# x and the output moved in two transfers each, the first of a multiple of 16 rows, and a ninth buffer for x

## The chip, the cores and the metric

The kernel runs on one core of a Trainium2 chip. A core has a matrix engine (TensorE, PE in the profile, with its weight load as PEld), a vector engine (DVE), a scalar engine (ACT), GpSimd (POOL), and SyncE (SP), which here only issues transfers. Sixteen DMA engines move data between the chip's main memory (HBM) and the core's on-chip memory (SBUF). Each engine works off its own list of instructions in the order in which the program was built; engines wait for each other through semaphores. A DMA is issued by one engine's queue (SP, ACT or POOL) and then runs by itself.

The metric is the device time of one execution in microseconds, less is better.

## The reference

A decoder trunk with two layers over 16 learned meta tokens followed by 1024 tokens of x, model width 1024, all in float32. Layer 0 is a Mamba-2 mixer and a gated feed-forward with a short causal convolution; layer 1 is stick-breaking attention and the same kind of feed-forward. What stands at the two ends matters here:

```python
def reference(x, meta_tokens, ...):
    h = jnp.concatenate([meta_tokens[None], x], axis=1)        # 1040 rows of 1024
    ...
    h = h + _ssd_mixer(_rmsnorm(h, ssd_norm[layer]), ...)
    h = h + _conv_ffn(_rmsnorm(h, ffn_norm[layer]), ...)
    ...
    h = h + _stick_breaking_attention(q, k, v) @ sb_w_o
    h = h + _conv_ffn(...)
    return _rmsnorm(h, final_norm)[:, N_META:]                 # 1024 rows of 1024
```

## The kernel before

**Tiles.** The 1040 rows are cut into nine chunks `CH`: eight of 116 rows and a last one of 112. Three chunks make a token tile `TT` of 348 (or 344) columns. A chunk sits in SBUF with its rows on the partitions, 4 KB to a row. The first chunk is made of the 16 meta rows and 100 rows of x, so its load from x has 100 rows, and so has its store.

**The start (`load_x`, L279 to L350).** For each chunk a tile `x` is taken from a pool with `XB` buffers (L292, L51), and its load is issued on SP for odd chunks and on ACT for even ones (L293 to L297). The weight for dt (`w_dt`, L299) is loaded after the first chunk. Then `ORD` (L50) sets six steps in order: `stream` of token tile 0, `stream` of 1, `scaled` of 0 and so on.

- `stream(j)` squares its three chunks and sums each row (L316 on DVE for the chunks in `SQD`, that is 1, 4 and 7; L318 on ACT for the others). Then it goes through eight column blocks k: three transposes on TensorE (L323), a copy to `h` by ACT or DVE in turn (L326, L328), and the product for dt (L329), which the profile shows as a pair of matmuls. In token tile 2 each finished row block of `h` is stored to `h_d` on SP (L331). `token_rstd` (L195 to L209) makes 1/rms for each row.
- `scaled(j)` multiplies the three chunks by their 1/rms in place (L340), transposes them again (L345), and splits each result into a high and a low part (L256, L257). A chunk's buffer is free after its `scaled`.

The projections of the mixer follow: `load_w` (L135) loads a weight tile of 512 KB on SP (L138), splits it on ACT (L144) and POOL (L145), and `mm3` makes three matmuls for each pair of tiles (L151 to L153; in the projections their output is `pj`).

**The end (`finish`, L1419 to L1471).** It is called for each token tile when its rows of the last feed-forward are complete. It transposes the chunks back (L1432), multiplies by 1/rms and the gain (L1466 with L1467, or L1469), and stores each chunk of `y` on SP (L1471). For the last token tile the squares are taken after the transposes (L1450 to L1457).

**What sets the order.** Outside two stretches that are ordered by hand (the chunks of the state-space mixer and the attention), a planner sets the order of the instructions on each engine when the program is built: it runs the program through a simulated time line and writes down the order that comes out. SP's order, with all its transfers, comes from it in the whole program. The programs of before and after are each planned anew.

Of the kernel before, what the change touches and what calls it, by code (L numbers as in the profile page):

```python
# [16 lines left out]
META = 16  # L17
# [30 lines left out]
SUMS = ((6, 1), (3, 6), (7, 6), (3, 5), (5, 7)), ((4, 7), (2, 1))  # L48
LPOOL = ((2, 2), (2, 4), (2, 6), (2, 7))
ORD = ((0, 0), (1, 0), (0, 1), (1, 1), (0, 2), (1, 2))  # L50
XB, SQD = 8, (1, 4, 7)  # L51
SCALE = 0.125


# [12 lines left out]
class Trunk:  # L67
# [211 lines left out]
    def load_x(self, pool, mx):  # L279

        nc, a = self.nc, self.a
        H = HEADS
        ss = self.cp.tile([P, 9], F32, tag="ss0", name="ss0")
        nc.vector.memset(ss, 1.0)
        wdt = self.wp.tile([P, 1024], F32, tag="w32", name="wdt")
        self.ln_exp()
        d = self.dp.tile([KD, P, L], F32, tag="h0_d", name="h0_d")
        r9 = mx.tile([P, 3, 3], F32, tag="r9", name="r9")
        dt = self.ex("dtr")
        xs = []  # L290
        for c, (t0, n) in enumerate(CH):
            xt = pool.tile([P, D], F32, tag="x", name=self.nm("x"), bufs=XB)  # L292
            if c == 0:  # L293
                nc.sync.dma_start(xt[:META, :], a["meta"])
                nc.scalar.dma_start(xt[META:n, :], a["x"][: n - META, :])
            else:
                (nc.sync if c % 2 else nc.scalar).dma_start(xt[:n, :], a["x"][t0 - META : t0 - META + n, :])  # L297
            if c == 0:
                nc.sync.dma_start(wdt[:, : KD * H], a["w_dt"])  # L299
                v = wdt[:, : KD * H].rearrange("p (k h) -> p k h", k=KD)  # L300
                nc.gpsimd.tensor_tensor(v, v, self.par("ssd_norm", 0, KD).unsqueeze(2).to_broadcast([P, KD, H]), op=ALU.mult)
            xs.append(xt)
        u = [(self.Q("uh", F32R), self.Q("ul", F32R)) for _ in range(KD)]
        for t in (t for hl in u for t in hl):
            nc.gpsimd.tensor_copy(t[:, :HALO], self.zero)
        hs = [self.Q("h") for _ in range(KD)]

        def stream(j):
            s0, nn = TT[j]
            x3 = xs[3 * j : 3 * j + 3]  # L310
            for i in range(3):
                c = 3 * j + i
                n = CH[c][1]
                t = self.wp.tile([P, D], F32, tag="wl", name=self.nm("junk"))
                if c in SQD:
                    nc.vector.scalar_tensor_tensor(t[:n, :], x3[i][:n, :], 1.0, x3[i][:n, :], op0=ALU.mult, op1=ALU.mult, accum_out=ss[:n, c : c + 1])  # L316
                else:
                    nc.scalar.activation(t[:n, :], x3[i][:n, :], AF.Square, accum_out=ss[:n, c : c + 1])  # L318
            for k in range(KD):
                ps = self.lg("xT")  # L320
                for i in range(3):
                    n = CH[3 * j + i][1]
                    nc.tensor.transpose(ps[:, i * CB : i * CB + n], x3[i][:n, k * P : k * P + P], self.ident[:n, :n])  # L323
                h = hs[k][:, s0 : s0 + nn]
                if k % 2:
                    nc.scalar.activation(h, ps[:, :nn], AF.Copy)  # L326
                else:
                    nc.vector.tensor_copy(h, ps[:, :nn])  # L328
                nc.tensor.matmul(dt[j * H : j * H + H, :nn], wdt[:, k * H : k * H + H], h, start=k == 0, stop=k == KD - 1)  # L329
                if j == 2:  # L330
                    nc.sync.dma_start(d[k], hs[k][:, :L])  # L331
            self.token_rstd(ss[:, 3 * j : 3 * j + 3], CB, 3, y=r9[:, :, j])

        def scaled(j):
            s0, nn = TT[j]
            x3 = xs[3 * j : 3 * j + 3]
            for i, t in enumerate(x3):
                n = CH[3 * j + i][1]
                r = r9[:n, i : i + 1, j]
                nc.vector.tensor_scalar(t[:n, :], t[:n, :], r, None, op0=ALU.mult)  # L340
            for k in range(KD):
                ps = self.sm("xr")
                for i in range(3):
                    n = CH[3 * j + i][1]
                    nc.tensor.transpose(ps[:, i * CB : i * CB + n], x3[i][:n, k * P : k * P + P], self.ident[:n, :n])  # L345
                self.parts(ps[:, :nn], u[k], s0, nn, self.par("ssd_norm", k))

        for step, j in ORD:
            (scaled if step else stream)(j)
        return d, u, dt, r9  # L350

    def spill(self, rows, name):
        d = self.dp.tile([len(rows), P, L], F32, tag=name, name=name)
        for k, t in enumerate(rows):
            self.nc.gpsimd.dma_start(d[k], t[:, :L])
        return d
# [1062 lines left out]
    def finish(self, h, j):  # L1419
        nc, out = self.nc, self.a["out"]  # L1420
        if j == 0:
            self.gfin = self.wp.tile([P, D], F32, tag="w32", name="gfin")
            nc.sync.dma_start(self.gfin, self.a["final_norm"].to_broadcast([P, D]))
        s0, n = TT[j]
        chunks = [(i, *CH[3 * j + i]) for i in range(3)]
        ss = self.small("fs")
        banks = cycle((self.sm,) if j < 2 else (self.lg, self.mm, self.lg, self.ex, self.mm, self.ex))

        def flip(t0, m, b):
            p = next(banks)("fin")  # L1430
            for k in range(4):
                nc.tensor.transpose(p[:m, k * P : k * P + P], h[4 * b + k][:, t0 : t0 + m], self.ident)  # L1432
            return p

        if j < 2:
            accs = self.square_sum([h[k][:, s0 : s0 + n] for k in range(KD)], n, D)
            pss = self.sm("fs")
            for i, _, m in chunks:
                for x, acc in enumerate(accs):
                    nc.tensor.matmul(pss[:m, i : i + 1], acc[:, i * CB : i * CB + m], self.one, start=x == 0, stop=x == 1)  # L1440
            nc.vector.tensor_copy(ss[:CB, 0:3], pss[:CB, 0:3])
            r = self.token_rstd(ss, CB, 3, 0.0)
            flipped = {}
        else:
            s2 = self.cp.tile([P, 2, 4], F32, tag="fs2", name="fs2")
            nc.vector.memset(s2, 0.5 * D)
            flipped = {(i, b): flip(t0, m, b) for i, t0, m in chunks for b in range(2)}
            for i, _, m in chunks:
                for b in range(2):
                    p, q = flipped[i, b], self.wp.tile([P, D], F32, tag="wl", name=self.nm("junk"))[:m, :512]  # L1450
                    if b:
                        c = self.wp.tile([P, D], F32, tag="wh", name=self.nm("copy"))
                        nc.vector.tensor_copy(c[:m, :512], p[:m])
                        p = flipped[i, b] = c[:, :512]
                        nc.vector.scalar_tensor_tensor(q, p[:m], 1.0, p[:m], op0=ALU.mult, op1=ALU.mult, accum_out=s2[:m, b, i : i + 1])
                    else:
                        nc.scalar.activation(q, p[:m], AF.Square, accum_out=s2[:m, b, i : i + 1])  # L1457
            nc.vector.tensor_tensor(ss[:, :3], s2[:, 0, :3], s2[:, 1, :3], op=ALU.add)
            r = self.token_rstd(ss, CB, 3)
        for i, t0, m in chunks:  # L1460
            y = self.Q("y")[:, :D]
            for b in range(2):
                w = slice(512 * b, 512 * b + 512)
                p = flipped.get((i, b)) or flip(t0, m, b)
                if b and i < 2:
                    nc.scalar.activation(y[:m, w], p[:m], AF.Copy, scale=r[:m, i : i + 1])  # L1466
                    nc.gpsimd.tensor_tensor(y[:m, w], y[:m, w], self.gfin[:m, w], op=ALU.mult)  # L1467
                else:
                    nc.vector.scalar_tensor_tensor(y[:m, w], p[:m], r[:m, i : i + 1], self.gfin[:m, w], op0=ALU.mult, op1=ALU.mult)  # L1469
            s = META if t0 == 0 else 0  # L1470
            nc.sync.dma_start(out[t0 + s - META : t0 + m - META, :], y[s:m, :])  # L1471

    def run(self, ctx):
        tc = self.tc
# [84 lines left out]
```

## Time and profile before

| | us |
|---|---|
| median of 3 runs | 3035.69 |
| lowest and highest run | 3035.06, 3035.73 |
| the profiled execution | 3036.55 |
| its span, first to last instruction | 3034.8 |

Over the span TensorE is busy 95% (2885.8 us), its weight loads 91%, DVE 76%, ACT 54% and POOL 43%. The transfers moved 273.42 MB at a mean of 90 GB/s; the queue of SP carried 258.54 MB of that and the queue of ACT 6.56 MB.

The span is the profiler's, from the first to the last instruction; the execution's own time is 1.75 us longer. In the lines of the profile, `out<-in` names the tile written and the tiles read, `x3` counts instructions, and brackets give the idle time of the engine before the instruction and what ended it. A line that starts with two numbers has the start and the length in us. `SPq` and `ACTq` stand for transfers issued on those engines' queues: their time is that of the issue, not of the transfer. A line of the waits has who waited, for whom, the sum in us, how often, and the longest.

### The profile page before, as it was taken

Reading aid. Unit: us, or ns where it says so; the run is one execution under the profiler, and the core shown is the slowest. Engines: PE = TensorE matmul, PEld = TensorE weight load, DVE = VectorE, ACT = ScalarE, POOL = GpSimd, SP = SyncE. Lnnn points to the kernel's source line nnn. Section 1 sums busy time; section 2 is a strip of 40 time slices with the busy share of each in tenths; the row PEclk is TensorE's granted clock in tenths of the full one; section 3 lists DMA queues with packets and bytes.
Section 4 is the critical chain, followed back from the end, with each engine's and each line's share of the span. In section 5 each row is a group of like instructions: output and inputs, shape, how many; then the busy total and the mean of one; then the engine's idle time right before and its main releaser. Section 6 shows DMA issues by size and latency. Waiting matters only on the chain.

```text
span 3034.8 us, 58705 instructions
## 1 busy us (share of the span) xinstructions
PE 2885.8 (95%) x22535; PEld 2773.6 (91%) x22535; DVE 2307.4 (76%) x4062; ACT 1650.2 (54%) x3403; POOL 1310.5 (43%) x1257
## 2 busy tenths in 40 slices
PE   5999999989998999999999999999898999999997
PEld 2999898979998999998999999999798999999996
DVE  3677868886459878878876888888749888778874
ACT  2555545553235555565334888888736555655332
POOL 1154434452234766663443222222344666663441
PEclk8999999999999999999999999999999999999998
DMA  3333333323222222225232222221332222225231
GB/s 109 112 95 89 109 91 104 98 81 129 63 79 74 74 81 78 77 87 187 72 122 85 56 68 59 70 63 52 135 107 72 83 78 75 81 86 188 77 99 56
DMA packets 123221, 273.42 MB, mean 90 GB/s; under 512 B 13468, under 2 KB 53020, under 8 KB 122940
## 3 DMA queue, kind: packets, MB, share of 16 engines
q1 hardware_dynamic: 117622, 258.54, 27.6%
q10 hardware_dynamic: 4054, 6.56, 0.6%
q8 instruction: 177, 2.90, 0.4%
q0 software_dynamic: 1264, 4.57, 0.4%
q14 instruction: 104, 0.85, 0.1%
HBM read 201.25 MB, written 53.45 MB: 84 GB/s over the span
## 4 chain that ended last, share of the span: by engine, by line
PE 43%; DVE 7%; issue 2%; ACT 1%; POOL 0%; DMA 0%; POOLq 0%; DVEq 0%; ACTq 0%
PE p L152 5%; PE p L151 5%; PE p L153 5%; PE acc L152 4%; PE acc L153 4%; PE acc L151 4%; PE pj L151 3%; PE pj L153 3%; PE pj L152 3%; PE po L1329 3%; PE lg L1288 2%; PE wT L1315 2%; DVE gl L1025 2%; PE ms L801 0%; DVE p L1041 0%
## 5 line engine op out<-in xcount | busy, mean ns | idle before, releaser
L151 PE MATMUL pj<-uh,wh 128*128 128x348 f32 (+2 forms) x1536 | 505.1, 329 | 9.3 <-ACT bk L602 6.5
L152 PE MATMUL pj<-ul,wh 128*128 128x348 f32 (+2 forms) x1536 | 496.6, 323 | 0.0
L153 PE MATMUL pj<-uh,wl 128*128 128x348 f32 (+2 forms) x1536 | 494.9, 322 | 0.7 <-POOL wl L1180 0.7
L151 PE MATMUL p<-bh,fh 128*128 128x262 f32 x1408 | 403.8, 287 | 6.6 <-DVE c L276 4.5
L153 PE MATMUL p<-bh,fl 128*128 128x262 f32 x1408 | 403.0, 287 | 3.6 <-POOL fl L875 3.6
L152 PE MATMUL p<-bl,fh 128*128 128x262 f32 x1408 | 402.3, 286 | 0.1
L875 POOL TENSOR_TENSOR fl<-x,fh 128x1024 fp32r<-128x1024 f32 x88 | 212.5, 2416 | 269.6 <-ACT fh L874 174.1
L152 PE MATMUL p<-bl,wh 128*128 128x262 f32 x1056 | 303.1, 287 | 6.2 <-DVE bl L827 6.1
L151 PEld LDWEIGHTS pj<-uh,wh 128*128 128x128 f32 x1536 | 291.2, 190 | 15.1 <-issue 4.8
L151 PE MATMUL p<-bh,wh 128*128 128x262 f32 x1056 | 302.4, 287 | 0.9 <-ACT bh L826 0.9
L145 POOL TENSOR_TENSOR wl<-w,wh 128x1024 fp32r<-128x1024 f32 (+2 forms) x76 | 155.2, 2044 | 341.0 <-ACT wh L144 340.9
L153 PE MATMUL p<-bh,wl 128*128 128x262 f32 x1056 | 301.3, 285 | 0.0
L276 DVE SCALAR_TENSOR_TENSOR c<-p,params,c 128x260 f32<-128x260 f32 x528 | 251.6, 483 | 56.2 <-ACT c L273 46.6
L152 PEld LDWEIGHTS pj<-ul,wh 128*128 128x128 f32 x1536 | 291.6, 190 | 1.4 <-issue 0.7
L153 PEld LDWEIGHTS pj<-uh,wl 128*128 128x128 f32 x1536 | 291.0, 189 | 1.1 <-POOL wl L1180 1.0
L151 PEld LDWEIGHTS p<-bh,fh 128*128 128x128 f32 x1408 | 268.8, 191 | 7.5 <-ACT c L273 4.9
L153 PEld LDWEIGHTS p<-bh,fl 128*128 128x128 f32 x1408 | 268.4, 191 | 4.1 <-POOL fl L875 4.0
L152 PEld LDWEIGHTS p<-bl,fh 128*128 128x128 f32 x1408 | 268.7, 191 | 0.8 <-DVE bl L827 0.5
L152 PE MATMUL acc<-gl,wh 128*128 128x260 f32 x896 | 255.1, 286 | 11.7 <-DVE gl L1025 11.7
L151 PE MATMUL acc<-gh,wh 128*128 128x260 f32 x896 | 251.0, 285 | 8.8 <-DVE p L1070 7.6
L153 PE MATMUL acc<-gh,wl 128*128 128x260 f32 x896 | 253.6, 285 | 0.0
L916 DVE TENSOR_TENSOR c<-c,c 128x260 f32<-128x260 f32 x176 | 240.7, 1370 | 4.9 <-ACT c L912 1.9
(324 smaller groups left out, 8436.8 us busy)
## 6 DMA issues: line engine op xcount, KB each, us to landing
w<-in_w_up SPq DMA_DIRECT2D x88, 512.0 KB
g<-c SPq DMA_DIRECT2D x176, 130.0 KB
w<-in_w_down SPq DMA_DIRECT2D x44, 512.0 KB
w<-in_w_in SPq DMA_DIRECT2D x40, 512.0 KB
b<-g SPq DMA_DIRECT2D x32, 520.0 KB
E<-ea_d SPq DMA_DIRECT2D x32, 464.0 KB
D<-acs_d SPq DMA_DIRECT2D x32, 420.5 KB
h<-h_d SPq DMA_DIRECT2D x16, 520.0 KB
```

The source lines that it names most:

```text
L145: nc.gpsimd.tensor_tensor(wl[:, :n], w32[:, :n], wh[:, :n].bitcast(F32), op=ALU.subtract)
L151: mm(out, wh, uh, start=first, stop=False, skip_group_check=joins)
L152: mm(out, wh, ul, start=False, stop=False, skip_group_check=joins)
L153: mm(out, wl, uh, start=False, stop=last, skip_group_check=joins)
L276: nc.vector.scalar_tensor_tensor(out, ps[:, o + i : o + i + n], wcol(i), out, op0=ALU.mult, op1=ALU.add)
L875: tt(lo[:, :n], t, hi[:, :n].bitcast(F32), op=ALU.subtract)
L916: self.last_up = tt(g[:, :FN], g[:, :FN], v[:, :FN], op=ALU.mult)
L1025: tt(gl, x, gh.bitcast(F32), op=SUB)
L1288: nc.tensor.matmul(ps[:nt, :m], part[:, c0 : c0 + nt], ks[a][:, s0 : s0 + m], start=x == 0, stop=x == 1)
L1315: nc.tensor.transpose(pt[:ns, x * CB : x * CB + nt], bt[a][:nt, x * CB : x * CB + ns], self.ident[:nt, :nt])
L1329: nc.tensor.matmul(po[64 * a : 64 * a + 64, :nt], v[: CH[c][1], c, 64 * a : 64 * a + 64], wt[a][: CH[c][1], c, :nt], start=x == 0, stop=x ...
```

## The change

Each load of a chunk of x and each store of a chunk of the output is made by a helper `by_rows`, which issues a first transfer of the largest multiple of 16 rows and a second one of the rows left, on the same queue. For 116 rows these are 112 and 4, for the 100 rows of the first chunk 96 and 4; the 112 rows of the last chunk make one transfer. The pool of x tiles has nine buffers in place of eight, one for each chunk; a buffer takes 4 KB of each partition.

```diff
-XB, SQD = 8, (1, 4, 7)
+XB, SQD = 9, (1, 4, 7)
...
-                nc.scalar.dma_start(xt[META:n, :], a["x"][: n - META, :])
+                self.by_rows(nc.scalar, xt[META:n, :], a["x"][: n - META, :], n - META)
             else:
-                (nc.sync if c % 2 else nc.scalar).dma_start(xt[:n, :], a["x"][t0 - META : t0 - META + n, :])
+                self.by_rows(nc.sync if c % 2 else nc.scalar, xt[:n, :], a["x"][t0 - META : t0 - META + n, :], n)
...
+    def by_rows(self, eng, dst, src, n):
+
+        m = n // 16 * 16
+        for r in (slice(0, m), slice(m, n)):
+            if r.start < r.stop:
+                eng.dma_start(dst[r], src[r])
...
-            nc.sync.dma_start(out[t0 + s - META : t0 + m - META, :], y[s:m, :])
+            self.by_rows(nc.sync, out[t0 + s - META : t0 + m - META, :], y[s:m, :], m - s)
```

## The prediction

> **What bounds the kernel now.** I read the page's slices first, then the windows of the first 92 us and of the end, then the timeline of each engine there, then the waits.
>
> ```profile
> span 3034.8 us, 58705 instructions
> PE   5999999989998999999999999999898999999997
> ```
>
> TensorE (PE) is at 90% or more nearly everywhere, so only work on its path counts. It is thin in the first slice (75.9 us) and in the last. Windows (columns: stretch, its length, busy us and instructions of PE, weight load, DVE, ACT, POOL, then granted clock, DMA share, GB/s):
>
> ```profile
> 10.00:22.00 12.00, 3.44 (x10) 1.52 (x11) 1.74 (x4) 1.61 (x3) 0.62 (x1) 1.00 0.26 104
> 22.00:28.00 6.00, 1.50 (x5) 0.34 (x3) 1.18 (x2) 0.00 (x0) 0.00 (x0) 0.87 0.82 203
> 28.00:42.00 14.00, 5.28 (x12) 1.51 (x12) 1.67 (x10) 4.75 (x12) 0.00 (x0) 0.50 0.26 103
> 42.00:63.00 21.00, 17.95 (x83) 8.55 (x83) 15.48 (x24) 7.62 (x14) 5.67 (x2) 0.88 0.02 7
> 63.00:67.00 4.00, 0.59 (x7) 0.37 (x5) 0.99 (x2) 0.65 (x2) 0.00 (x0) 1.00 0.39 115
> 67.00:92.00 25.00, 24.85 (x136) 17.59 (x136) 10.90 (x24) 12.78 (x26) 2.36 (x1) 0.93 0.70 255
> ```
>
> From 10 to 42 us no compute engine is busy, and the DMA share stands at 0.26 with 104 GB/s: about four of sixteen engines, full. From 42 to 63 PE works, with DVE close behind (15.48 of 21); at 63 a second hole opens; from 67 PE is full. What the holes wait for:
>
> ```profile
> DVE junk L316 <- DMA x<-in_x: 26.8, 3, 16.7
> 6.55 1.06 ACT L318 ACTIVATE junk<-x 116x1024 f32<-116x1024 f32 x1 [4.46 <-DMA x<-in_x]
> 16.09 1.06 ACT L318 ACTIVATE junk<-x 116x1024 f32<-116x1024 f32 x1 [8.39 <-DMA x<-in_x]
> 17.83 1.23 DVE L316 SCALAR_TENSOR_TENSOR junk<-x 116x1024 f32<-116x1024 f32 x1 [16.68 <-DMA x<-in_x]
> 41.96 1.23 DVE L316 SCALAR_TENSOR_TENSOR junk<-x 116x1024 f32<-116x1024 f32 x1 [2.88 <-DMA x<-in_x]
> 63.05 0.33 ACTq L297 DMA_DIRECT2D x<-in_x  x1
> 66.90 1.06 ACT L318 ACTIVATE junk<-x 112x1024 f32<-112x1024 f32 x1 [2.93 <-DMA x<-in_x]
> 65.00:66.00 1.00, 0.00 (x0) 0.00 (x0) 0.00 (x0) 0.00 (x0) 0.00 (x0) 1.00 0.77 299
> ```
>
> The first square of each x tile shows its landing: tile 0 at 6.5, tile 2 at 16.1, tile 1 at 17.8, tile 7 at 42.0. The ninth tile is issued only at 63.05 (ACT's own queue), when a buffer is free. It has 112 rows and 448 KB, and is there 3.85 us later, moved at 299 GB/s. Tiles of 116 rows move at 104. That contrast is the case for the change.
>
> **The change, part by part.** It adds a second transfer of four rows to eight loads and to eight stores; the ninth load and store have 112 rows and stay whole. The compute instructions are the same. The sums stand against the profiled execution's 3036.55 us, 0.86 above the median of the runs (3035.69).
>
> *Loads.* The share of 0.26 is four engines for 116 rows; 112 rows reached 0.77 in one microsecond. The Trainium skill, DMA: Bandwidth & Descriptors, section "Why a DMA increments its semaphore by 16 and not by 1", says a transfer uses the largest number of engines up to 16 that divides its outermost size: 4 for 116 rows, 16 for 112, 4 for the four rows left. By that rule, the trace agrees. The price needs a rate with more engines: below, 203 GB/s (22 to 28 us, weights mixed with x); above, 424 GB/s:
>
> ```profile
> 75.00:76.00 1.00, 1.00 (x9) 0.70 (x7) 0.00 (x0) 0.70 (x2) 0.32 (x1) 1.00 1.06 424
> params<-in_params POOLq DMA_DIRECT2D x1, 272.0 KB, 8.8
> 2.00:3.00 1.00, 0.00 (x0) 0.00 (x0) 0.00 (x0) 0.09 (x1) 1.00 (x6) 1.00 0.42 78
> ```
>
> I take 299, the one row of an x load. The engines start at about 2.5 us (share 0.42 from 2 to 3). Up to the first three tiles 1792 KB move (rows of 4 KB: meta 64, x 400 + 464 + 464; then w_dt's 128, 128 x 256 floats, and the parameters' 272): 1.835 MB / 299 GB/s = 6.1 us, so landed at 8.6 (6.8 to 11.5) in place of 17.8. All nine tiles are 4.67 MB: 18.1 us (13.5 to 25.5); tile 7 a tile earlier, 16.6. The four-row parts add 8 x 4 KB on each of four engines, 1.3 us at 26 GB/s (104 / 4), inside those bounds.
>
> Then the work begins that was hidden behind the loads. TensorE's transposes and its products for dt go eight times round in the first stage:
>
> ```profile
> 19.60 1.34 PE L329 MATMUL dtr<-h,wdt 128*32 128x348 f32 x2 [0.79 <-issue]
> 21.64 1.37 PE L329 MATMUL dtr<-h,wdt 128*32 128x348 f32 x2
> 43.01 1.02 PE L329 MATMUL dtr<-h,wdt 128*32 128x348 f32 x2
> 44.40 0.77 PE L329 MATMUL dtr<-h,wdt 128*32 128x348 f32 x2
> 45.55 0.77 PE L329 MATMUL dtr<-h,wdt 128*32 128x348 f32 x2
> 11.89 12.33 SPq L138 DMA_DIRECT2D w<-in_w_in  x2
> 43.23 1.06 ACT L144 ACTIVATE wh<-w 128x1024 fp32r<-128x1024 f32 x1 [1.72 <-DMA w<-in_w_in]
> ```
>
> One round takes 2.04 us unhindered (19.60 to 21.64), 1.15 later (44.40 to 45.55). The sixth pair, at 43.01, is my mark. Afterwards the first pair comes 1.8 us after the third tile, as now (17.8 to 19.6), at 10.4; five rounds of 2.04 put the mark at 20.6. The row at 43.23 is the guard: ACT waits for the first weight tile, which stands behind the x loads in SP's queue (issue from 11.9); it would land at about 18.1 + 0.52 MB / 299 = 19.9, so it no longer holds the mark back. I count 21: **22 us gained**. Bounds: rounds of 1.15 and 424 GB/s give 14.3, but tile 7's square stands before the mark on DVE, so 15.5 (27.5 gained); at 203 GB/s the weight tile comes at 28 (15 gained). From the mark to 63 the rows show work, not waiting, so this part keeps its 20 us.
>
> *The ninth buffer.* Tile 8's load no longer waits for tile 0's buffer and lands with the rest. PE idled 3.41 us there:
>
> ```profile
> 66.92 0.41 PE L323 MATMUL xT<-ident,x 112*128 112x112 f32 x2 [3.41 <-DMA x<-in_x]
> 69.00:70.00 1.00, 1.00 (x4) 0.50 (x4) 0.10 (x1) 0.97 (x4) 0.00 (x0) 0.50 1.00 404
> ```
>
> Below, that 3.41; above, 5.5, since the granted clock fell to 0.50 behind the hole for some microseconds. I take **4**. What is next late is TensorE itself (24.85 of 25 us from 67 to 92), so nothing swallows the shift.
>
> *Stores.* Six of nine lie inside the last feed-forward, behind PE work; cover gone, each would cost its issue on SP, 0.32 us (the row at 3019.40). The last three end the program:
>
> ```profile
> 3017.44 3.05 POOL L1467 TENSOR_TENSOR y<-y,gfin 116x512 f32<-116x512 f32 x2 [16.06 <-ACT y L1466]
> 3019.40 0.32 SPq L1471 DMA_DIRECT2D out<-y  x1
> 3020.52 1.77 SPq L1471 DMA_DIRECT2D out<-y  x1
> 3019.00:3022.00 3.00, 0.00 (x0) 0.00 (x0) 0.37 (x1) 0.00 (x0) 1.49 (x1) 0.50 0.65 142
> 3022.00:3033.00 11.00, 0.00 (x0) 0.00 (x0) 0.00 (x0) 0.00 (x0) 0.00 (x0) 0.50 0.26 88
> 3033.00:3034.00 1.00, 0.00 (x0) 0.00 (x0) 0.00 (x0) 0.00 (x0) 0.00 (x0) 0.50 0.04 16
> ```
>
> Compute ends at 3020.5; the 11 us from 3022 are a quarter of the engines, emptying two tiles of 116 rows. The bytes end at about 3033.4, the span 1.4 later. Afterwards 1.41 MB (464 + 448 + 464 KB) run from 3019.5: at 299 GB/s to 3024.2, and 0.3 for the last four-row issue, so the span ends at 3025.9 (8.9 gained). At 142 / 0.65 = 218 GB/s, the store rate of this place, 7.1; at 424, the last tile's own trip limits, 10.2. I take **8**.
>
> *Sum:* 22 + 4 + 8 = 34; 3036.55 - 34 = 3002.6, and 3035.69 - 34 = 3001.7 against the median: 3002. With all low ends 25.5 (3011), with all high ends 43 (2993).
>
> *What the added transfers wait for.* SP's fourth x load waited for another x load:
>
> ```profile
> SPq L297 <- DMA x<-in_x: 3.2, 1, 3.2
> 4.01 0.26 ACTq L297 DMA_DIRECT2D x<-in_x  x1
> ```
>
> It is the tenth queued transfer of the program, and moved when the second had landed (6.5); the ninth, on ACT, issued at 4.0. I read this as at most eight in flight. Split, eight are four tiles, so later loads wait for landings, and on ACT the squares and copies queue behind them, then PE behind ACT. At 3.85 us a trip this costs little; the price where it does is the first rival.
>
> **The rivals.** *ACT is held by its own loads.* Tiles 4, 6 and 8 issue on ACT, and each part waits for an earlier landing. If two such trips follow the 4.0 us of today, and last 6 us instead of 3.85, ACT is free at 16; squares and copies begin there and the mark comes at about 30. Gain 13 + 4 + 8 = 25: 3011, and to 3018 if the ninth load also stays late. For it: the waits above. Against: a trip of 3.85.
>
> *The planner writes another order.* The order on each engine comes from simulated times, and more transfers can move other work. SP is in order: if the first weight tile goes behind the h_d stores, as the third one now does, projections start some 10 us late. That gives 3012; a better order, 2990. For it: SP's wait for h_d held it 38.8 us. Against: TensorE has transposes to do meanwhile.
>
> ```profile
> SPq L331 <- DVE h L328: 47.5, 4, 38.8
> 69.29 0.40 SPq L138 DMA_DIRECT2D w<-in_w_in  x1
> ```
>
> *Splitting brings no engines, only trips: slower.* Each large part still moves at 104 GB/s, and each small part follows as a trip of its own. The fixed part of a trip is 3.85 - 0.459 MB / 299 GB/s = 2.3 us. Eight loads one after the other give 18.4 us, the last store 2.3; less the 4 of the buffer, 17 slower: 3053. It decides below about 170 GB/s, where 0.475 MB / 170 + 2.3 - 4 / 8 reaches today's 4.6 us for a tile (0.475 / 104). Against it stands the 112-row load at 299 GB/s. The Trainium skill, same page, section "Rules for kernel authors", speaks on this side: two transfers to disjoint partition halves serialize, one whole transfer is better. By that rule, 3053; no 116-row load here shows it.
>
> **How the numbers follow.** Forecast 0.73 (3002); ACT held 0.13 (3011); another order 0.09 (3012, some of it faster); no engines, only trips 0.05 (3053). The range 2993 to 3018 takes the forecast's bounds and the two middle rivals, and leaves out the last and extremes of the others. A measurement of this kernel tells about 0.2%, 6 us, from no change: faster 0.94; 0.02 within, from an order that gives all back; slower 0.04, nearly all of the last rival.
>
> **What would show it.** Right: DMA share above 0.6 from 3 to 18 us and no plateau at 0.26; the sixth dtr pair near 21; no hole before the 112-row square; pj products dense from about 41 in place of 67; bytes of the last stores ending near 3024. Wrong: ACT's first square after 12 us (first rival); w's first conversion late on SP (second); a plateau at 0.26 again (third). If the start shifts and the total does not, the dense stretch gave it back.

## The result and the profile after

| | before | after |
|---|---|---|
| median, four runs each (us) | 3035.38 | 3009.47 |
| lowest and highest | 3034.76 to 3035.73 | 3005.55 to 3010.49 |
| the profiled execution | 3036.55 | 3009.70 |
| its span | 3034.8 | 3008.0 |

The ratio is 0.9912 (95%: 0.9898 to 0.9925): the kernel is some 26 us faster, where 34 were forecast. The profiled executions differ by 26.85 us, and the sections below say where these come from.

The page of after, its span and its slices. The first slice of PE, 75.2 us long, rose from 5 to 7, the last from 7 to 8:

```profile
span 3008.0 us, 58728 instructions
...
PE   7999999989998999999999999999898999999998
```

The windows of the start (columns as before: PE, weight load, DVE, ACT, POOL, granted clock, DMA share, GB/s):

```profile
2.00:6.00 4.00, 0.30 (x2) 0.29 (x2) 0.00 (x0) 0.09 (x1) 3.44 (x23) 1.00 0.95 261
6.00:14.00 8.00, 3.21 (x10) 1.14 (x9) 1.66 (x3) 0.00 (x0) 0.62 (x1) 1.00 1.04 268
14.00:22.00 8.00, 4.59 (x13) 1.43 (x11) 2.66 (x9) 6.39 (x15) 0.00 (x0) 1.00 1.03 269
22.00:36.00 14.00, 11.02 (x45) 4.37 (x44) 11.79 (x21) 6.14 (x13) 5.11 (x2) 0.91 0.33 101
36.00:92.00 56.00, 54.89 (x329) 43.07 (x328) 34.05 (x63) 32.37 (x56) 7.40 (x3) 0.99 0.29 105
```

The share of 0.95 to 1.04 says that all sixteen engines now work from 2 to 22 us, at 261 to 269 GB/s (a share can come out a little over 1, since a packet's whole time counts where it starts); the plateau of 0.26 with 104 GB/s is gone. But look at ACT: nothing at all from 6 to 14. PE is full from 36 us, where it was from 67. The timeline of the same stretch says why ACT did nothing, and when the first products come (rows of ACT's queue, ACT and PE, by time; the other rows are left out):

```profile
0.83 14.35 ACTq L357 DMA_DIRECT2D x<-in_x  x9
...
12.35 1.34 PE L329 MATMUL dtr<-h,wdt 128*32 128x348 f32 x2 [0.47 <-issue]
...
15.29 1.06 ACT L318 ACTIVATE junk<-x 116x1024 f32<-116x1024 f32 x1 [13.20 <-DMA x<-in_x]
...
17.87 1.37 PE L329 MATMUL dtr<-h,wdt 128*32 128x348 f32 x2 [3.41 <-ACT h L326]
...
23.52 1.06 ACT L318 ACTIVATE junk<-x 112x1024 f32<-112x1024 f32 x1 [1.81 <-DMA x<-in_x]
...
25.16 0.77 PE L329 MATMUL dtr<-h,wdt 128*32 128x348 f32 x2 [0.19 <-ACT h L326]
```

ACT issues nine parts of x, and these issues take until 15.18; its first square is at 15.29. The bracket there names the DMA of x, because that semaphore came last by the profile, but what held ACT is the row above it: an engine that issues transfers does its work behind them. PE then waits 3.41 us for ACT's copy before the second pair of dtr products. The sixth pair, the mark of the prediction, is at 25.16 (before 43.01): 17.85 us earlier, not 22. A pair takes 1.34 to 1.37 us up to the fourth and 0.77 from the fifth: TensorE is at half clock until then. The windows' 1.00 is no measurement there, since the clock's record in this trace begins only at 23.2 us and what lies ahead of it counts as full. The 112-row tile is squared at 23.52 (before 66.90), and PE has no hole ahead of it.

The end, in the timeline and in windows:

```profile
2979.35 23.94 SPq L357 DMA_DIRECT2D out<-y  x11
...
2999.18 3.05 POOL L1474 TENSOR_TENSOR y<-y,gfin 116x512 f32<-116x512 f32 x2 [16.11 <-ACT y L1473]
```

```profile
3002.00:3003.00 1.00, 0.00 (x0) 0.00 (x0) 0.00 (x0) 0.00 (x0) 0.23 (x1) 0.50 0.84 279
3003.00:3004.00 1.00, 0.00 (x0) 0.00 (x0) 0.00 (x0) 0.00 (x0) 0.00 (x0) 0.50 0.99 299
...
3006.00:3007.00 1.00, 0.00 (x0) 0.00 (x0) 0.00 (x0) 0.00 (x0) 0.00 (x0) 0.50 0.10 37
```

GpSimd's last product ends at 3002.23, the bytes at about 3006, the span at 3008.0: a tail of 5.8 us. Before, the same product ended at 3020.49 and the span at 3034.8: 14.3 us. The stores brought 8.5.

So 17.85 at the mark and 8.5 at the tail make 26.4 of the 26.85, and next to nothing is left of the 4 us of the ninth buffer. It did take its hole away; another one opened at 120 us. First before, then after, in the timeline of DVE and PE:

```profile
137.77 1.87 DVE L571 TENSOR_SCALAR D<-D,cols 116x116 f32<-116x116 f32 x8 [4.92 <-DMA D<-acs_d]
...
140.28 0.40 PE L151 MATMUL pj<-uh,wh 128*128 128x352 f32 x1 [1.62 <-DVE xbc L276]
140.51 0.33 PE L152 MATMUL pj<-ul,wh 128*128 128x352 f32 x1
```

```profile
116.76 1.60 DVE L578 TENSOR_SCALAR D<-D,cols 116x116 f32<-116x116 f32 x8 [9.04 <-DMA D<-acs_d]
...
120.22 0.63 PE L151 MATMUL pj<-uh,wh 128*128 128x348 f32 x1 [4.20 <-DVE xbc L276]
120.65 0.49 PE L152 MATMUL pj<-ul,wh 128*128 128x348 f32 x1
```

D is the decay matrix of the state-space mixer's first chunk. DVE works in order: it stands at D until D's transfer has landed, and behind it stand the conv taps (L276, the steps of the mixer's short convolution) that read the projections' results out of TensorE's output tiles, so PE runs out of tiles to write. DVE stood 4.92 us before and 9.04 after; PE's hole grew from 1.62 to 4.20. And the product behind the first one takes 0.49 us in place of 0.33: the clock is at half for a while (0.66 over 117 to 127 us, in a window shown further down).

How the lead over before develops is best seen by the start of one and the same matmul in both traces (counted back from the last one; from 525 us on PE's order is the same, but for some sixty matmuls near 948 us in buf9_alone): dt's transposes (L396, in after L403) lead by 23.5 us, the first D operation by 21.0, the matmul at 525 us of before by 19.4, the last matmul by 18.3. The table has this for every kernel tried; the idle time is the sum of the times without a matmul in the first 160 us, "taps" are the conv taps that stand ahead of the first D operation in DVE's list, and "hole at D" is PE's idle time ahead of the product that waits for the taps behind D.

| kernel | median us | PE idle in the first 160 us | taps | hole at D | lead at 525 us | lead at the last matmul |
|---|---|---|---|---|---|---|
| before | 3035.4 | 39.7 | 35 | 1.62 | 0 | 0 |
| after (nine_again: a second time) | 3009.5, 3011.0 | 22.2, 21.7 | 33 | 4.20, 4.30 | 19.4, 18.8 | 18.3, 20.5 |
| stores_alone | 3027.5 | 38.8 | 35 | 1.62 | 0.1 | 0.5 |
| loads_buf9 | 3017.4 | 22.5 | 33 | 4.38 | 21.2 | 20.0 |
| by_columns | 3047.0 | 47.4 | 30 | 5.76 | -10.5 | -12.1 |
| buf9_alone | 3044.7 | 46.6 | 30 | 5.96 | -7.4 | -12.6 |
| rows_buf8 (eight_again: a second time) | 3005.0, 3004.9 | 19.3, 18.6 | 36 | 1.54, 1.09 | 22.6, 24.8 | 23.5, 25.9 |
| acs_first | 3009.5 | 22.2 | 33 | 3.64 | 19.0 | 19.9 |
| dt_earlier | 3007.2 | 19.3 | 35 | 1.75 | 22.7 | 16.1 |
| rest_on_pool | 3023.3 | 37.0 | 30 | 6.23 | 4.2 | 4.7 |
| x_on_sp | 2998.9 | 16.3 | 35 | 1.62 | 31.3 | 29.6 |
| sp_buf8 | 3010.6 | 23.0 | 37 | 2.26 | 15.7 | 13.0 |

The lead at 525 us follows the idle time saved at the start: it stands between 3 us below it (by_columns) and 8 above (x_on_sp). The fewer taps ahead of D, the longer the hole there, in all but sp_buf8. After 525 us most kernels keep their lead within 3 us; buf9_alone and dt_earlier lose 5 to 7, and for both the profiled run is the longest of its kernel.

### The profile page after: what moved, and what is told of

It is laid out like the page before. It is cut to its first block, busy times and chain, and to the rows that moved or that the text cites. A ratio compares the mean times of both kernels' runs of the same rounds, so it can differ in the third digit from the quotient of the medians.

```text
span 3008.0 us, 58728 instructions
## 1 busy us (share of the span) xinstructions
PE 2886.3 (96%) x22535; PEld 2776.1 (92%) x22535; DVE 2304.7 (77%) x4062; ACT 1653.0 (55%) x3405; POOL 1306.0 (43%) x1257
## 5 line engine op out<-in xcount | busy, mean ns | idle before, releaser
L276 DVE SCALAR_TENSOR_TENSOR c<-p,params,c 128x260 f32<-128x260 f32 x528 | 251.5, 483 | 57.2 <-ACT c L273 47.5
```

The costliest lines, as they stand in the source:

```text
L276: nc.vector.scalar_tensor_tensor(out, ps[:, o + i : o + i + n], wcol(i), out, op0=ALU.mult, op1=ALU.add)
```

## The experiments

Each edit is against the changed kernel. The median of before on the same chip was 3034.58 beside stores_alone, loads_buf9, by_columns and buf9_alone, 3037.38 beside acs_first, x_on_sp, rest_on_pool and rows_buf8, 3035.21 beside dt_earlier and sp_buf8, and 3035.16 beside nine_again and eight_again.

### The parts alone: stores

The loads whole and eight buffers, so only the stores are split:

```diff
-XB, SQD = 9, (1, 4, 7)
+XB, SQD = 8, (1, 4, 7)
...
-                self.by_rows(nc.scalar, xt[META:n, :], a["x"][: n - META, :], n - META)
+                nc.scalar.dma_start(xt[META:n, :], a["x"][: n - META, :])
...
-                self.by_rows(nc.sync if c % 2 else nc.scalar, xt[:n, :], a["x"][t0 - META : t0 - META + n, :], n)
+                (nc.sync if c % 2 else nc.scalar).dma_start(xt[:n, :], a["x"][t0 - META : t0 - META + n, :])
```

> Split stores alone; loads in one transfer, eight buffers. Theory: the last bytes end about 5.8 us after GpSimd's last product instead of 14.3, so 8.5 less: 3027, with the start as before. Rival (the end was bounded by the write's own completion, and the shorter tail came with the shifted start): 3034 to 3036.

Measured: 3027.52 (ratio 0.9980, 0.9967 to 0.9992). Timeline and window of its end:

```profile
3016.93 3.05 POOL L1474 TENSOR_TENSOR y<-y,gfin 116x512 f32<-116x512 f32 x2 [16.07 <-ACT y L1473]
```

```profile
3020.00:3024.00 4.00, 0.00 (x0) 0.00 (x0) 0.00 (x0) 0.00 (x0) 0.00 (x0) 0.50 0.86 277
```

The compute ends where it did (3019.98 against 3020.49), and the tail to the end of the span at 3025.7 is 5.7 us in place of 14.3. The order of PE, DVE and ACT is that of before here. The term of the stores by itself is 8.6 us by the tails and 7.1 by the medians; the interval of the ratio allows 2.4 to 10.

### The parts alone: loads with nine buffers

```diff
-            self.by_rows(nc.sync, out[t0 + s - META : t0 + m - META, :], y[s:m, :], m - s)
+            nc.sync.dma_start(out[t0 + s - META : t0 + m - META, :], y[s:m, :])
```

> Split loads and nine buffers, stores in one transfer: the complement. Theory: 3009.5 + 8.5 = 3018, sixth dtr pair at 25, the tail again 14 us with 11 us at a DMA share of a quarter. If the parts do not add up (the sum of this gain and that of the split stores is not 26 within 3), something in the middle depends on both.

Measured: 3017.43 (0.9941, 0.9919 to 0.9962). Its last product ends at 3000.46 and its span at 3014.7, so the tail is 14.2 again. The parts hardly touch each other: 7.1 us by the stores alone (3034.58 - 3027.52) and 17.2 by the loads with the ninth buffer (3034.58 - 3017.43) make 24.2, and the whole change has 25.9 (3035.38 - 3009.47).

### Does a second transfer help, or the number of rows?

Two transfers of all rows, each of 512 columns, in place of two by rows (the loads and the stores):

```diff
-        m = n // 16 * 16
-        for r in (slice(0, m), slice(m, n)):
+        m = D // 2
+        for r in (slice(0, m), slice(m, D)):
             if r.start < r.stop:
-                eng.dma_start(dst[r], src[r])
+                eng.dma_start(dst[:, r], src[:, r])
```

> As many transfers as the change makes, but cut by columns: two of 116 rows by 512 columns, nine buffers. Theory (row count sets the engines): share stays at 0.26 in the loads and at the end, so 3030 to 3036, like the ninth buffer alone or a little worse by the added issues. Rival (two transfers in place of one are what brings the speed, whatever their rows): near 3010.

Measured: 3047.02 (1.0036, 1.0025 to 1.0047), slower than before. A window, and the row of ACT's queue:

```profile
6.00:22.00 16.00, 4.25 (x12) 1.72 (x12) 2.19 (x4) 0.00 (x0) 0.62 (x1) 1.00 0.26 98
```

```profile
0.83 26.35 ACTq L357 DMA_DIRECT2D x<-in_x  x10
```

The plateau of 0.26 is back, at 98 GB/s with two transfers of 116 rows. So it isn't the second transfer that brings the engines; it is the row count. The ten issues hold ACT until 27.2, later than in any other kernel here; the theory had the share right, but its time of 3030 to 3036 was too short. How much of the loss is the issues' and how much the ninth buffer's this run alone doesn't tell; the next one, on the same chip, has the buffer without the added transfers and loses nearly as much.

### The ninth buffer alone

Loads and stores in one transfer each, nine buffers:

```diff
-        m = n // 16 * 16
+        m = n
```

> Ninth buffer alone, every load and store in one transfer. Theory (rows set the number of DMA engines, and that is nearly all of the gain): the loads keep the 0.26 share to about 44 us, only the hole before the 112-row tile goes (3.4 to 5.5 us of 26): 3030 to 3032. Rival (the buffer carries the start, the split only the end): about 3017, and the sixth dtr pair still near 43 but no loss behind it.

Measured: 3044.66 (1.0028, 1.0016 to 1.0039). Neither theory had it slower. Timeline of ACT's queue and of PE:

```profile
0.83 9.19 ACTq L357 DMA_DIRECT2D x<-in_x  x5
...
110.35 0.63 PE L151 MATMUL pj<-uh,wh 128*128 128x352 f32 x1 [4.59 <-DVE xbc L276]
...
143.24 0.63 PE L151 MATMUL pj<-uh,wh 128*128 128x348 f32 x1 [5.96 <-DVE xbc L276]
```

The hole ahead of the 112-row tile is gone here too, but there are two holes of 4.59 and 5.96 us behind conv taps that before doesn't have (by_columns has them too, with 4.60 and 5.76), and only 30 taps stand ahead of D in place of 35. The buffer does what it says; the order that the planner writes with it costs more. This took the theory of a free 4 us down and raised the next question: does it cost with split loads too?

### Eight buffers, loads and stores split

```diff
-XB, SQD = 9, (1, 4, 7)
+XB, SQD = 8, (1, 4, 7)
```

> The split of loads and stores with eight buffers. Theory: the last tile again waits for the first buffer, a hole of about 3.4 us plus some half clock: 3012 to 3016. Rival (with fast loads the ninth buffer is worth nothing, since TensorE has other work by then): 3009 to 3011.

Measured: 3004.95 (0.9896, 0.9883 to 0.9910), below what both the theory and the rival gave. By the median it is 4.5 below the change, but not beside it on one chip, and the two intervals overlap. So both kernels were timed on one chip:

> The changed kernel itself, timed on one chip beside the same with eight buffers, since the two medians so far (3009.5 and 3005.0) come from separate chips and their intervals overlap. Theory (the order that the planner writes with nine buffers costs TensorE about 3 us of holes and half clock in the first 530 us, lead 19.4 against 22.6): 3 to 5 us slower than the eight-buffer kernel. Rival (the difference is the chip and the drift of the granted clock after 530 us): within 2 us of it, either way.

> The changed kernel with eight buffers, on the chip of the run beside it. Theory: 3003 to 3007 and 3 to 5 us faster than nine buffers. Rival: within 2 us of nine buffers, either way.

Measured: nine 3010.95 (3007.69 to 3015.53), eight 3004.87 (3001.01 to 3009.26). With the eight runs that each has by now, the means are 3010.0 and 3005.4, and the difference of 4.6 us has a 95% interval from 1.4 to 7.8 (on the one chip alone it is 6.1 by the medians, but the times of the two kernels still overlap there). The ninth buffer, with the order that comes with it, costs time here as well. The timeline of PE in rows_buf8:

```profile
44.25 0.64 PE L323 MATMUL xT<-ident,x 112*128 112x112 f32 x2 [3.26 <-DMA x<-in_x]
...
122.13 0.40 PE L151 MATMUL pj<-uh,wh 128*128 128x348 f32 x1 [1.54 <-DVE xbc L276]
```

The hole ahead of the last tile is back with 3.26 us, and the hole at D is 1.54 in place of 4.20: one hole stands against the other, with a smaller one elsewhere (the dtr pairs wait 2.54 us for ACT, not 3.41, as ACT has one issue less and is free at 11.29 us in place of 15.18).

This kernel also gives the split of the loads without the ninth buffer. Against stores_alone, which differs from it in the loads and the order that comes with them, its lead at the last matmul is 23 us larger (23.5 - 0.5). At the mark 18.3 of that is there (43.01 - 24.71).

### Is D late because its rows are stored late?

D is loaded from a buffer in HBM that is written just before. Here the rows of `acs_d`, that D needs, are stored ahead of those of `ea_d`; only SP's order changes:

```diff
-        for j in range(3):
-            for d, t in ((self.acs_d, rows), (self.ea_d, ea)):
+        for d, t in ((self.acs_d, rows), (self.ea_d, ea)):
+            for j in range(3):
```

> The change, with the three stores of acs_d written ahead of the three of ea_d in the program; only the order of these six transfers on SP differs, every compute engine's order is the same. Theory (after 100 us TensorE runs ahead into a wait for the first D tile, whose load stands behind ea_d, and the hole and the half clock after it give back about 6 us): D lands 2 to 4 us earlier, the 4.2 us hole shrinks to under 2, total 3003 to 3006. Rival (the give-back is something else, such as how transfers fall in the later stages): 3008 to 3011.

Measured: 3009.51 (0.9915, 0.9899 to 0.9931), no different from the change. The hole is 3.6 us, and D comes at 115.4 in place of 116.8, but measured from the dt steps before it only 0.6 us sooner. A miss: the order of the stores isn't the lever.

### More taps ahead of D

The steps that make dt and, from it, the rows that D is loaded from (the dt steps) are drawn into the first projections one block earlier; nine buffers and the loads stay:

```diff
-                if n % 3 == 2:
+                if n % 3 == 1:
                     next(dt, None)
```

> The changed kernel (nine buffers, split loads and stores) with one number changed in the order of the first projections: the dt steps are drawn one block earlier (n % 3 == 1 in place of 2), which leaves 35 in place of 33 conv taps ahead of the first D operation on DVE. Theory (the hole of TensorE at 120 us comes from how many taps stand ahead of D on DVE, and its price is the hole and the half clock behind it): the hole shrinks from 4.2 to about 1.6 us, the half-clock windows behind it go, and the time is 3003 to 3006 in place of 3009.5. Rival (the hole is given back later, or the loss after 100 us comes from elsewhere): the hole shrinks and the time stays at 3008 to 3011.

Measured: 3007.15 (3004.69 to 3011.91; 0.9909, 0.9896 to 0.9923). The timeline of PE, and the window behind the hole, first of this kernel, then of after:

```profile
118.39 0.40 PE L151 MATMUL pj<-uh,wh 128*128 128x352 f32 x1 [1.75 <-DVE xbc L276]
```

```profile
117.00:127.00 10.00, 8.61 (x54) 8.64 (x55) 6.45 (x14) 6.26 (x11) 0.00 (x0) 1.00 0.47 135
```

```profile
117.00:127.00 10.00, 6.78 (x27) 6.81 (x28) 6.39 (x17) 6.11 (x9) 0.00 (x0) 0.66 0.53 152
```

The hole and the half clock behind it went as the theory said: 54 matmuls in these 10 us in place of 27, and a lead at 525 us of 22.7, as with eight buffers, in place of 19.4. Yet the time lies between what the theory and the rival gave, and its interval holds the change's ratio of 0.9912. The profiled run (3011.91, the longest of the four) lost 6.6 us of its lead after 525 us. So one number in the order took the hole at D away, and with it came some 3 us up to 525 us; that closing it makes the whole kernel faster isn't shown.

### ACT without the loads

All loads of x on SP, nine buffers, nothing else:

```diff
-                self.by_rows(nc.scalar, xt[META:n, :], a["x"][: n - META, :], n - META)
+                self.by_rows(nc.sync, xt[META:n, :], a["x"][: n - META, :], n - META)
...
-                self.by_rows(nc.sync if c % 2 else nc.scalar, xt[:n, :], a["x"][t0 - META : t0 - META + n, :], n)
+                self.by_rows(nc.sync, xt[:n, :], a["x"][t0 - META : t0 - META + n, :], n)
```

> The change, with all loads of x issued on SP. Theory (ACT is held by its own nine issues to 15.2 us, and this is what the start fell short by): ACT's first square comes near 8 us, the second dtr pair no longer waits 3.4 us, sixth pair at 21 to 22: 3 to 4 us less at the mark, total 3005 to 3008 if the later stages keep it. Rival (the loads themselves are the limit): sixth pair at 25 again, 3009 or slower, as SP's queue becomes longer.

Measured: 2998.87 (2994.87 to 3001.10; 0.9872, 0.9857 to 0.9888), faster than the change by more than both intervals, and below the theory's range. Timeline of SP's queue, ACT and PE:

```profile
2.53 14.70 SPq L357 DMA_DIRECT2D x<-in_x  x15
...
5.70 1.06 ACT L318 ACTIVATE junk<-x 116x1024 f32<-116x1024 f32 x1 [3.61 <-DMA x<-in_x]
...
14.63 1.34 PE L329 MATMUL dtr<-h,wdt 128*32 128x348 f32 x2 [0.47 <-issue]
...
18.72 0.77 PE L329 MATMUL dtr<-h,wdt 128*32 128x348 f32 x2 [0.28 <-DVE h L328]
...
22.46 0.77 PE L329 MATMUL dtr<-h,wdt 128*32 128x348 f32 x2
...
109.71 0.40 PE L151 MATMUL pj<-uh,wh 128*128 128x352 f32 x1 [1.62 <-DVE xbc L276]
```

SP is held as ACT was, but SP has nothing else to do. ACT squares at 5.70 and PE doesn't wait for it: six pairs take 7.83 us from the first to the sixth, where after needs 12.81. The first pair is later (14.63 against 12.35), the sixth 2.7 us earlier. Of the 5 us between 7.83 and 12.81, 3.41 are the wait for ACT; the rest is the clock, since a pair takes 0.77 us from the third on, where after has 1.37 and 1.35 for its third and fourth. The windows of the first 180 us of before, after and this kernel add the rest:

```profile
0.00:180.00 180.00, 140.30 (x814) 113.15 (x815) 90.72 (x186) 79.19 (x133) 36.64 (x43) 0.93 0.32 102
```

```profile
0.00:180.00 180.00, 157.81 (x941) 130.68 (x942) 106.16 (x224) 92.10 (x150) 46.05 (x49) 0.97 0.38 112
```

```profile
0.00:180.00 180.00, 163.73 (x1052) 139.31 (x1054) 114.13 (x248) 94.88 (x157) 52.00 (x52) 1.00 0.40 120
```

The clock's 0.97 in after is 5.4 us at most (180 x 0.03), here it is nothing; PE idles 5.9 us less (22.2 - 16.3). Both together nearly make the 11.9 us that it leads after by at 525 us (31.3 - 19.4). Only 2.7 of these are there at the mark; the others come with an order that has 35 taps ahead of D and a hole of 1.62. The Trainium skill, DMA: Bandwidth & Descriptors, section "Issuing engines are not separate DMA queues", says that issuing from several engines saves only the time of the issue, as all transfers run on the same DMA engines. The trace agrees in the main: one queue alone carries 238 GB/s from 6 to 14 us and 257 from 14 to 22, against 268 and 269 with two. What the move saves ACT is the time of its issues.

### Fewer issues on ACT, the other way

The four-row parts go to GpSimd's queue, so ACT issues five transfers and SP four:

```diff
-                self.by_rows(nc.scalar, xt[META:n, :], a["x"][: n - META, :], n - META)
+                self.by_rows(nc.scalar, xt[META:n, :], a["x"][: n - META, :], n - META, nc.gpsimd)
...
-                self.by_rows(nc.sync if c % 2 else nc.scalar, xt[:n, :], a["x"][t0 - META : t0 - META + n, :], n)
+                self.by_rows(nc.sync if c % 2 else nc.scalar, xt[:n, :], a["x"][t0 - META : t0 - META + n, :], n, nc.gpsimd)
...
-    def by_rows(self, eng, dst, src, n):
+    def by_rows(self, eng, dst, src, n, rest=None):
...
-        for r in (slice(0, m), slice(m, n)):
+        for e, r in ((eng, slice(0, m)), (rest or eng, slice(m, n))):
             if r.start < r.stop:
-                eng.dma_start(dst[r], src[r])
+                e.dma_start(dst[r], src[r])
```

> The change, with the four-row parts of the loads issued on GpSimd's queue. Theory (at most eight transfers of SP and ACT are in flight, so the split makes later loads wait for earlier ones): with nine fewer in that count ACT's issues end before 8 us in place of 15.2, sixth dtr pair 2 to 4 us earlier. Rival (ACT's issues are slow for another reason, such as full rings): issues end near 15 again and the pair stays at 25.

Measured: 3023.31 (0.9953, 0.9940 to 0.9967), 14 us slower than the change. Timeline of ACT's queue, ACT and PE:

```profile
0.83 5.90 ACTq L357 DMA_DIRECT2D x<-in_x  x5
...
23.41 1.06 ACT L144 ACTIVATE wh<-w 128x1024 fp32r<-128x1024 f32 x1 [12.11 <-DMA w<-in_w_in]
...
25.62 1.04 ACT L318 ACTIVATE junk<-x 116x1024 f32<-116x1024 f32 x1
...
34.68 0.77 PE L329 MATMUL dtr<-h,wdt 128*32 128x348 f32 x2
```

ACT is free of its issues at 6.73, as expected. But the planner then put the split of the first weights ahead of five of the six squares in ACT's list, and ACT waits for these weights until 23.41; the sixth pair comes at 34.68. Only 30 taps stand ahead of D, too. A small change of the loads moved the order, and the order cost more than the earlier end of ACT's issues gave: this is the prediction's second rival, in another place.

### Both: SP and eight buffers

```diff
-XB, SQD = 9, (1, 4, 7)
+XB, SQD = 8, (1, 4, 7)
```

on top of the kernel with all loads on SP.

> All loads of x on SP, split, but with eight buffers for x. 37 conv taps stand ahead of the first D operation, against 35 with nine buffers on SP. Theory (eight buffers won beside loads on ACT only because of the order at D, which is already good with loads on SP): the hole at D stays at about 1.5 us, the hole ahead of the 112-row tile comes back with 3 to 5 us, and the time is 3001 to 3005 in place of 2998.9. Rival (eight buffers are better by themselves, whatever queue the loads use): 2994 to 2997.

Measured: 3010.57 (0.9918, 0.9904 to 0.9931). The timeline of PE:

```profile
18.93 1.37 PE L329 MATMUL dtr<-h,wdt 128*32 128x348 f32 x2 [0.26 <-DVE h L328]
...
24.77 0.77 PE L329 MATMUL dtr<-h,wdt 128*32 128x348 f32 x2
...
48.70 0.64 PE L323 MATMUL xT<-ident,x 112*128 112x112 f32 x2 [3.28 <-DMA x<-in_x]
...
127.84 0.40 PE L151 MATMUL pj<-uh,wh 128*128 128x352 f32 x1 [2.26 <-DVE xbc L276]
```

The hole ahead of the last tile is back as expected, the one at D grew a little, and the time is worse than the theory's range of 3001 to 3005. With the loads on SP the ninth buffer gains about 12 us (2998.87 against 3010.57, on two chips, the intervals of the ratios apart); with loads on both queues it costs 4.6, with whole loads 10 (3044.66 - 3034.58). What it costs or gains depends on the kernel around it, then, and each of these kernels got an order of its own. The buffer itself, with the order held, wasn't run.

The run also limits what the experiment with nine buffers says of ACT. ACT is as free here, with its first square at 5.57 us, and no pair waits long for it. But the pairs still take 1.37 us at 18.93, and the sixth comes at 24.77, no sooner than with eight buffers on both queues (24.71). By the medians this kernel is 5.6 us slower than rows_buf8 (3010.57 against 3004.95), where with nine buffers the move to SP gained 10.6. So the wait behind ACT's issues is gone with the loads on SP, in both kernels; that this makes the kernel faster is shown for nine buffers only.

## Why the prediction held, and where it didn't

| term | forecast | found |
|---|---|---|
| start of the loads, at the sixth dtr pair | 22 (15 to 27.5) | 17.85 (43.01 to 25.16) |
| ninth buffer, from the mark to the last matmul | 4 (3.4 to 5.5) | 0.5 (18.3 - 17.85) |
| stores, at the tail | 8 (7.1 to 10.2) | 8.5 (14.3 - 5.8) |
| sum | 34 | 26.85 |

The time lies inside the range of 2993 to 3018, but nearer to the two middle rivals (3011 and 3012) than to the forecast of 3002, and something of both rivals was at work. The prediction's own sign of the first one came true: ACT's first square is at 15.29 us, after 12. Of its signs of being right, the share, the missing plateau and the missing hole ahead of the 112-row tile came true; the sixth pair near 21 didn't.

**More engines: right.** The share and the rate came as read from the one tile of 112 rows, with 261 to 269 GB/s against the 299 that the sum used, inside its bounds of 203 and 424. by_columns shows that the row count does it. That also takes down the third rival. The Trainium skill, DMA: Bandwidth & Descriptors, section "Rules for kernel authors", advises against two transfers to disjoint partition halves, since they serialize, and gives as its reason that each half uses all 16 engines anyway. Here the whole transfer doesn't (a share of 0.26), so the reason is missing, and the rival's 3053 didn't come. The Trainium skill, same page, section "Why a DMA increments its semaphore by 16 and not by 1", gives four engines for 116 rows and sixteen for 112. The traces agree, with 0.26 for whole tiles and for halves by columns, and 0.95 to 1.04 for the split. One reading was too strong: that no compute engine is busy from 10 to 42 us. The prediction's own rows have PE at 3.44 of 12 us and 5.28 of 14 there.

**The mark: right in its mechanism, 4.2 us late.** Two steps were off. "Afterwards the first pair comes 1.8 us after the third tile" put it at 10.4, and it came at 12.35; the step gave the engines to the first three tiles alone, with 1.835 MB, but by the time the third is there (11.23 us) they have moved 2.47 MB (268 GB/s over 9.23 us). Later tiles took their share, and one queue doesn't cure it (x_on_sp has its first pair at 14.63). And "at 3.85 us a trip this costs little" failed: nine issues held ACT to 15.18, and PE waited 3.41 us behind it. The round of 2.04 us, called unhindered, is a round at half clock (pairs of 1.34 and 1.37 us); that it fitted the rounds from 17.87 to 22.02 (2.07 and 2.08) is because the half clock lasted that long again. The first rival had this, with its mark at 30; so the mechanism of the rival ran inside the forecast's own case, at a smaller price. x_on_sp and sp_buf8 show that the wait is gone without issues on ACT; the mark is at 22.46 in the one and at 24.77 in the other, by the clock of the rounds.

**The ninth buffer: wrong.** The hole was taken away as forecast, and at the transposes of dt, at 77 us, the lead had grown from 17.85 to 23.5. The step that failed is "what is next late is TensorE itself (24.85 of 25 us from 67 to 92), so nothing swallows the shift". The row of 67 to 92 says nothing of what lies behind 92: at 120 us DVE stands at D, and how much PE has then depends on how many taps the planner put ahead of D. The shift was swallowed from there on: the lead is 21.0 at the first D operation and 19.4 at 525 us. rows_buf8, eight_again and nine_again put the term, with the order that comes with it, at -4.6 (-7.8 to -1.4) in this kernel, not at +4.

**The stores: right**, within half a us, and alone too (stores_alone).

**Another order: more likely than the 0.09 it got.** It was priced with one place, the first weight behind the h_d stores, which didn't come about (ACT's first split of a weight is at 25.01 us in after). It came at D instead. In every kernel here that changed a load or a buffer against before the order moved. Kernels that differ in one such thing lie up to 14 us apart by the medians (rest_on_pool against the change), and no run separates what of that is the order alone.

**What stays open.** Why the planner puts 33, 35 or 36 taps ahead of D wasn't tried, nor was the buffer tested with the order held fixed. And the number of taps isn't all of it: sp_buf8 has most of them (37) and a hole of 2.26. Why the clock rises at the third pair in x_on_sp and only at the sixth in sp_buf8 is open too, and so how much of the best time below is luck of the order.

The best version that was run is x_on_sp, the changed kernel with all loads of x on SP: 2998.87 us, 38.5 less than before on the same chip (3037.38).

## What to carry to other kernels

Read the DMA share of a stretch with nothing else in it: 0.26 of sixteen engines is four engines, and a transfer with a multiple of 16 rows (112 here) brings the others; the few rows left go in a second transfer. Look at which engine issues loads that come in a bunch: ACT stood at nine issues until 15.18 us, and all its work stood behind them. An engine that computes nothing is the place to try, but time it, since the same move gained 10.6 us with nine buffers and lost 5.6 with eight. And where a planner writes the order, a change of a buffer or a load is two changes, itself and a new order; look for the first place where an engine stands at work that waits for another chain, before you add a saved hole to the sum.

## What the runs showed of the hardware

**How long an issue holds its engine.** A free issue takes about 0.3 us (0.32 and 0.26 in the rows of the prediction). Five issues on ACT take 5.90 us (rest_on_pool), five whole ones 9.19 (buf9_alone), nine 14.35, ten slow ones 26.35 (by_columns): I read this as: the more transfers are under way, and the slower they are, the longer the next issue stands. That it is a limit of about eight under way was read from the counts; no run varied that limit.

**Which holes cost clock.** Among the projections, holes of 1.54, 1.62, 1.75 and 2.26 us were followed by a first product of 0.40 us and a full clock, and those of 4.20, 4.59 and 5.96 by a first product of 0.63. The one of 4.20 had about 7 us at half clock, some of it inside the hole (0.66 over ten). The first product isn't a safe sign: behind a hole of 4.38 it took 0.40, and the half clock came just after (loads_buf9):

```profile
119.49 0.40 PE L151 MATMUL pj<-uh,wh 128*128 128x348 f32 x1 [4.38 <-DVE xbc L276]
```

```profile
119.49:124.00 4.51, 4.51 (x19) 4.51 (x20) 3.24 (x6) 2.50 (x4) 0.00 (x0) 0.62 0.26 96
```

Nor is the length of the hole all: among the transposes of the start, one of 2.23 us, with one of 0.82 shortly ahead of it, was followed by half clock (before, ahead of 50.64):

```profile
50.64:53.64 3.00, 3.00 (x9) 1.59 (x10) 1.91 (x5) 1.43 (x3) 0.00 (x0) 0.50 0.00 0
```

A hole of 3.3 us had two prices in two runs of the same kernel, about 7 us at half clock and about half of that (windows of rows_buf8, then of eight_again):

```profile
44.00:51.00 7.00, 6.75 (x23) 3.95 (x24) 3.24 (x9) 3.46 (x9) 0.00 (x0) 0.51 0.71 246
```

```profile
44.00:51.00 7.00, 6.57 (x31) 4.45 (x32) 3.82 (x11) 3.91 (x10) 0.00 (x0) 0.76 0.70 255
```

PE had 23 matmuls in these 7 us in one run and 31 in the other. The Trainium skill, TensorE: Matmul & The Clock Gate, section "What's actually happening", has the array at half rate after an idle window of about 3.4 us. The trace agrees for the holes among the projections; the one of 2.23 us it doesn't fit as a plain length of idle time, and that the price of a 3.3 us hole depends on when it falls is my reading, which no run tests. It may be a part of the spread of this kernel, whose eight runs lie between 3005.55 and 3015.53 us.
